# A hybrid convolution and attention encoder layer on one core: loads in halves, a first third of one projection inside attention, a split last block, two softmax blocks on ScalarE

## The chip, the cores and the metric

The kernel runs on one core of one Trainium2 chip. The metric is the device time of one execution in microseconds (us), compared as the median of several runs. The engines are named as in the profile: PE is TensorE's matmul, PEld its weight load, DVE is VectorE, ACT is ScalarE, POOL is GpSimd, SP issues the DMAs. L162 means line 162 of the kernel before.

## The reference, cut to what matters

The layer takes 528 prompt rows (16 learned meta rows and 512 frames) and 32 sample rows, so 560 rows of 1024 features, all in float32.

```python
x = x + 0.5 * ((silu(h @ w_gate) * (h @ w_up)) @ w_down)      # h = rms_norm(x), D_FF = 2816
z = rms_norm(x) @ w_in_all        # conv B | C | v | q latent | kv latent | rotary key | 2 gates
conv_branch = (B * dwconv3_causal(C * v)) @ w_conv_out
s = q @ k.T * 96 ** -0.5          # 16 heads, masked by chunks of 64
p = softmax(s)
mla_branch = (p @ v) @ w_mla_out
x = x + (sigmoid(g_conv) * conv_branch + sigmoid(g_mla) * mla_branch) @ w_out_all
x = x + 0.5 * ((silu(h @ w_gate2) * (h @ w_up2)) @ w_down2)
```

The outputs are the two row groups after the second feed-forward step and the new convolution and key caches.

## The kernel before, in words

Activations lie with features on the 128 partitions and rows along the free axis; 1024 features are KD = 8 tiles. Every float32 operand of a product is split into a rounded high part (a cast on ACT, L116) and the rest (a subtraction on DVE or POOL, L117 and L73), and `mm3` (L161 to L165) makes three matmuls of each product: high by high, low by high, high by low. The weights come in column blocks of 128, 512 KB each, by `load` (L119): one DMA on SP's queue, the cast, the subtraction.

There are five stages in the program.

1. **The start** (L613 to L656) loads the rows with SP, transposes them on PE, scales them with ACT and DVE into `xh` and `xl`, and loads the first block of the gate and up weights in two halves with `load_early` (L144). SP's queue holds the DMAs in the order in which they stand there: gains, first 128 prompt rows, meta rows, sample rows, second 128 prompt rows, then the halves of the weights, then the other prompt rows. The transposes of the first 304 columns need the first two prompt tiles and the sample and meta rows.
2. **Feed-forward step 1**, `ffn` (L235).
3. **The mix stage**: 16 heads of attention (loop at L1160), and in between, as filler, the units of `stream` (L929): the conv and gate columns of `w_in_all` and the product with `w_conv_out`. `fill(us)` (L962) draws units from it. The gates and the conv branch go to DRAM (`gt_dram`, `cb_dram`). Per head, `score` makes the logits in PSUM, `soft` (L1093) takes the maximum on DVE and the exponential on ACT, L1189 to L1191 divide the four blocks `pv(t)` of 528, 400, 272 and 144 columns by their sums on DVE, L1226 and L1231 transpose the weights, L1242 and L1243 multiply them by the values into `ov`, and L1246 and L1247 add the two halves into `at`. `sample_values` (L1102) does the same for the sample rows of a pair of heads. The attention result of the last pair of heads goes straight into `vh` and `vl` (L1253), the others by DRAM (L1216 to L1219).
4. **The late stage** (L1297 to L1330): eight blocks `m` of the product with `w_mla_out` (PSUM tile `late`), each multiplied by a sigmoid of its gate and added to the gated conv branch, then the eight blocks of `w_out_all`. The first of these matmuls stand behind all 16 heads.
5. **Feed-forward step 2**, the same `ffn`. At its end `down` (L443) makes eight blocks `m` of the product with `w_down`; `close` (L472) adds block `m` to `y`, `done` (L1364) then calls `emit(m - 1)` (L1348), which transposes a finished block back on PE, copies it on ACT and DVE and stores it. Block 7 is emitted after its own `close`.

The program text does not fix each engine's order. The build's scheduler decides it from the text's order, the dependencies and its own costs of instructions; `add_manual_dep` with NOSYNC forbids it to put one instruction ahead of another. Each engine's queue is then fixed and runs in order. PSUM tags in the mix stage are `t`, `f`, `acc` (two banks each) and `s` (one tile of two banks).

## Time and profile before

| | |
|---|---|
| median of 3 runs | 1419.42 us (1417.48 to 1420.46) |
| profiled execution, its own time | 1418.22 us |
| its span in the trace | 1416.40 us |
| PE / PEld busy | 1381.2 us (98%) / 1352.1 us (95%) |
| DVE / ACT / POOL busy | 1012.8 / 648.8 / 441.4 us |
| chain that ended last | PE 85%, DVE 6%, DMA 4%, ACT 2% |
| DMA | 141.62 MB, mean 100 GB/s |

The span is what the trace covers from the first to the last instruction or transfer; the execution's own time has 1.8 us around it. A busy matmul is modelled with its pipeline's drain, so the distance between the starts of neighbouring matmuls tells their cost, not their durations.

### The profile page before, as it was taken

How to read it: one execution, taken by the hardware profiler on the slowest of the kernel's cores; microseconds unless marked ns; L12 is line 12 of the kernel's file. 1: busy time of each engine (PE TensorE's matmuls, PEld its weight loads, DVE VectorE, ACT ScalarE, POOL GpSimd, SP SyncE). 2: the span in 40 equal slices, each digit the busy share in tenths (PEclk: the TensorE clock that was granted, in tenths of full speed). 3: DMA queues.
4: the chain of work that ended last, by engine and by line, in shares of the span. 5: the costliest groups of instructions: out<-in, count | busy, mean ns of one | idle time of the engine just before them, and what ended most of it. 6: DMA issues, size and time to landing. Idle time of an engine off the chain costs nothing.

```text
span 1416.4 us, 26510 instructions
## 1 busy us (share of the span) xinstructions
PE 1381.2 (98%) x10615; PEld 1352.1 (95%) x10615; DVE 1012.8 (72%) x1740; ACT 648.8 (46%) x1202; POOL 441.4 (31%) x647
## 2 busy tenths in 40 slices
PE   7999999999999999999999999999999999999998
PEld 6999999999999999999999999899999999999998
DVE  5887878787576666856965877545877787878754
ACT  6644343435324355564554556543545253434341
POOL 1011111112396864654533434032811111111110
PEclk9999999999999999999999999999999999999999
DMA  6342323233243222222432244355533332423213
GB/s 174 90 119 66 115 75 105 85 95 90 89 125 95 85 80 78 72 61 65 124 96 81 77 138 134 110 184 155 143 90 107 88 113 67 119 69 112 85 46 97
DMA packets 215633, 141.62 MB, mean 100 GB/s; under 512 B 6415, under 2 KB 202914, under 8 KB 215510
## 3 DMA queue, kind: packets, MB, share of 16 engines
q1 hardware_dynamic: 215510, 139.93, 33.5%
q8 instruction: 83, 1.36, 0.4%
q14 instruction: 40, 0.33, 0.1%
HBM read 124.15 MB, written 15.76 MB: 99 GB/s over the span
## 4 chain that ended last, share of the span: by engine, by line
PE 85%; DVE 6%; DMA 4%; ACT 2%; issue 2%; POOL 1%; SPq 0%; DVEq 0%; POOLq 0%; ACTq 0%
PE acc L162 8%; PE acc L164 8%; PE b L162 8%; PE acc L163 8%; PE b L163 8%; PE b L164 8%; PE f L162 6%; PE f L163 6%; PE f L164 6%; PE late L162 2%; PE late L164 2%; PE late L163 2%; DMA wr<-in_ffn_w_down_dram 2%; PE t L1242 1%; PE t L1226 1%
## 5 line engine op out<-in xcount | busy, mean ns | idle before, releaser
L116 ACT CAST wh<-wr 128x1024 fp32r<-128x1024 f32 (+2 forms) x166 | 167.8, 1018 | 271.0 <-PE acc L163 127.9
L73 POOL TENSOR_TENSOR al<-tu,ah 128x187 fp32r<-128x187 f32 (+3 forms) x108 | 95.6, 913 | 572.2 <-issue 342.5
L162 PE MATMUL f<-xh,wh 128*128 128x272 f32 (+1 forms) x816 | 239.6, 294 | 3.4 <-DVE ext L891 1.4
L164 PE MATMUL f<-xh,wl 128*128 128x272 f32 (+1 forms) x816 | 238.0, 292 | 0.0
L163 PE MATMUL f<-xl,wh 128*128 128x272 f32 (+1 forms) x816 | 237.9, 292 | 0.1
L162 PE MATMUL acc<-ah,wh 128*128 128x280 f32 (+1 forms) x704 | 203.2, 291 | 1.7 <-ACT wh L116 1.3
L163 PE MATMUL acc<-al,wh 128*128 128x280 f32 (+1 forms) x704 | 203.9, 291 | 0.0
L164 PE MATMUL acc<-ah,wl 128*128 128x280 f32 (+1 forms) x704 | 202.7, 290 | 0.0
L73 POOL TENSOR_TENSOR wl<-wr,wh 128x256 fp32r<-128x256 f32 x196 | 152.5, 808 | 141.4 <-ACT wh L116 113.1
L117 DVE TENSOR_TENSOR wl<-wr,wh 128x1024 fp32r<-128x1024 f32 (+2 forms) x116 | 138.0, 1199 | 42.7 <-ACT wh L116 34.6
L162 PEld LDWEIGHTS f<-xh,wh 128*128 128x128 f32 x816 | 153.9, 189 | 4.7 <-ACT wh L116 1.6
L163 PEld LDWEIGHTS f<-xl,wh 128*128 128x128 f32 x816 | 154.1, 189 | 1.0 <-DVE xl L117 0.3
L164 PEld LDWEIGHTS f<-xh,wl 128*128 128x128 f32 x816 | 154.0, 189 | 0.6
L163 PE MATMUL b<-xsl,yh 128*128 128x272 f32 (+1 forms) x468 | 135.7, 290 | 0.0
L162 PE MATMUL b<-xsh,yh 128*128 128x272 f32 (+1 forms) x468 | 135.7, 290 | 0.0
L164 PE MATMUL b<-xsh,yl 128*128 128x272 f32 (+1 forms) x468 | 135.1, 289 | 0.0
L162 PEld LDWEIGHTS acc<-ah,wh 128*128 128x128 f32 x704 | 131.9, 188 | 2.7 <-ACT wh L116 1.7
L163 PEld LDWEIGHTS acc<-al,wh 128*128 128x128 f32 x704 | 132.5, 188 | 0.0
L164 PEld LDWEIGHTS acc<-ah,wl 128*128 128x128 f32 x704 | 132.0, 188 | 0.2 <-DVE wl L117 0.2
L117 DVE TENSOR_TENSOR yl<-ws,yh 128x1024 fp32r<-128x1024 f32 x78 | 100.6, 1289 | 8.3 <-ACT yh L116 8.0
L474 DVE SCALAR_TENSOR_TENSOR tu<-acc,R 128x560 f32<-128x560 f32 (+1 forms) x80 | 58.2, 729 | 46.4 <-PE acc L164 46.0
L162 PE MATMUL b<-xh,wh 128*128 128x272 f32 (+1 forms) x312 | 90.5, 290 | 0.0
(359 smaller groups left out, 3811.4 us busy)
## 6 DMA issues: line engine op xcount, KB each, us to landing
wr<-in_w_in_all_dram SPq DMA_DIRECT2D x43, 512.0 KB, 4.0
wr<-in_ffn_w_down_dram SPq DMA_DIRECT2D x32, 512.0 KB, 3.6
wr<-in_ffn_w_gate_dram SPq DMA_DIRECT2D x24, 512.0 KB, 4.4
wr<-in_ffn_w_up_dram SPq DMA_DIRECT2D x23, 512.0 KB, 4.6
wq<-in_ffn_w_up_dram SPq DMA_DIRECT2D x20, 512.0 KB, 5.6
wq<-in_ffn_w_gate_dram SPq DMA_DIRECT2D x19, 512.0 KB, 3.9
wr<-in_ffn_w_down_dram SPq DMA_DIRECT2D x16, 384.0 KB, 3.4
gt_dram<-b SPq DMA_DIRECT2D x16, 272.0 KB, 2.0
```

The costliest lines, as they stand in the source:

```text
L73: last = op(out[:, lo:hi], a[:, lo:hi], b[:, lo:hi])
L116: a = S.copy(hi, src)
L117: return a, (E or V).tensor_sub(lo, src, f(hi))
L162: first = PE.matmul(out, a[0], b[0], start=start, stop=False, skip_group_check=onto)
L163: PE.matmul(out, a[0], b[1], start=False, stop=False, skip_group_check=onto)
L164: PE.matmul(out, a[1], b[0], start=False, stop=stop, skip_group_check=onto)
L474: V.scalar_tensor_tensor(t, ps[:, :, :n], 0.5, Rv, op0=ALU.mult, op1=ALU.mult)
L1226: PE.transpose(ps[:, (t - j) * P : (t - j + 1) * P], pw[:, a : a + P], ident)
L1242: PE.matmul(ov[:, 512 - NT[j] :], vj, x, start=j == 0 and x is pTh[j], stop=j == NQ - 1 and x is pTl[j])
```

## The change

There are four edits. **The rows come in halves of 512 features**: `load_early` issues the sample, meta and first two prompt tiles' first halves ahead of the first halves of the weights, and their second halves ahead of the second halves of the weights. **A first third of the product with `w_mla_out` moves into the mix stage**: for the blocks m = 0, 1, 2 `first_outs` multiplies the seven finished tiles k of `vh`, `vl` into the mix stage's own PSUM banks `s`, `acc` and `f`, behind the filler; `last_outs` adds the eighth k once the last pair of heads is done, with a weight tile `w_last` of its own, and multiplies by the gates. Their six gates and conv tiles are loaded, and their sigmoids taken, before the last head's weights are transposed, and never ahead of the last exponential. The last pair's `sample_values` moves from behind that head's values to ahead of its transposes. **The last block of the last product is split** into 416 and 128 columns; the first part is closed and emitted while the second runs. **Two of the four softmax blocks** (528 and 400 columns) are divided on ACT.

```diff
+    def load_early(ws, rows):
...
         for k0, k1, E in ((0, KD // 2, V), (KD // 2, KD, GP)):
+            rows(k0 * P, k1 * P)
             for w, (raw, hi, lo) in zip(ws, tiles):
...
+                if last and finale and m == KD - 1:
+                    done(m)
+                    for q, (c0, c1) in enumerate(((0, N2 - P), (N2 - P, N2))):
+                        out = ps[:, q, : c1 - c0]
+                        for j in range(nf):
+                            ah, al = a[pairs[j // 2]]
+                            mm3(
...
+                        t = rows()[:, c0:c1]
+                        yc = y[:, m, lo + c0 : lo + c1]
+                        V.scalar_tensor_tensor(
+                            t, out, 0.5, R[:, lo + c0 : lo + c1], op0=ALU.mult, op1=ALU.mult
+                        )
+                        V.tensor_add(yc, yc, t)
+                        finale(m, q)
+                    return
...
-            dma(xp[:, 0], i["x_prompt"][0, :P])
-            dma(xm[:META], i["meta_tokens"])
-            dma(xm[META:MS], i["x_sample"][0])
-            dma(xp[:, 1], i["x_prompt"][0, P : 2 * P])
-            w0 = load_early([wg[:, :P], wu[:, :P]])
+            def first_rows(c0, c1):
+                dma(xm[META:MS, c0:c1], i["x_sample"][0, :, c0:c1])
+                dma(xm[:META, c0:c1], i["meta_tokens"][:, c0:c1])
+                for t in range(2):
+                    dma(xp[:, t, c0:c1], i["x_prompt"][0, t * P : (t + 1) * P, c0:c1])
+
+            w0 = load_early([wg[:, :P], wu[:, :P]], first_rows)
...
+        def first_outs():
+
+            for m in range(AHEAD):
+                w = load([w_mla(m)[: (KD - 1) * P]], E=GP)
...
+                for k in range(KD - 1):
+                    for q in range(2):
+                        x = slice(q * NL, (q + 1) * NL)
+                        x = mm3(ps[q], at_k(w, k), at_k((vh, vl), k, x), k == 0, False)
+                        if k == 0 and m:
+                            behind(x, turned[NQ if m > 1 else 0])
+                        yield 0.345
+
+        def last_outs():
+            for m, ps in sorted(enumerate(outs), key=lambda x: x[0] < 2):
+                for q in range(2):
+                    x = slice(q * NL, (q + 1) * NL)
+                    mm3(ps[q], at_k(w_last, 0, slice(m * P, (m + 1) * P)), at_k((vh, vl), KD - 1, x), False, True)
+                    V.tensor_mul(gates[m][:, x], ps[q], gates[m][:, x])
+                V.tensor_add(gates[m], gates[m], convs[m])
...
+        AHEAD = 3
...
             for t in range(NQ - 1, -1, -1):
-                V.tensor_scalar_mul(pv(t), pv(t), inv[:, t : t + 1])
-            soft(nm, sm, 4, pss[rows, :KP], pS[rows], rows)
+                if t >= NQ - 2:
+                    S.activation(pv(t), pv(t), AF.Identity, scale=inv[:, t : t + 1])
+                else:
+                    V.tensor_scalar_mul(pv(t), pv(t), inv[:, t : t + 1])
+            last = soft(nm, sm, 4, pss[rows, :KP], pS[rows], rows)
...
+            if h == HEADS - 1:
+                sample_values(VV, at, pS)
...
-        fill(1e9)
+        for _ in chain(filler, first_outs()):
+            pass
+
+        for m in range(AHEAD):
+            sc = back.tile([P, L], F32, tag=f"raw{m}", name="sc")
+            dma(sc, gt_dram[m])
+            behind(S.activation(sc, sc, AF.Sigmoid), last)
+            dma(convs[m], cb_dram[m])
+            GP.tensor_mul(convs[m], convs[m], sc)
+            dma(gates[m], gt_dram[KD + m])
+            behind(S.activation(gates[m], gates[m], AF.Sigmoid), last)
+        last_outs()
...
-        for m in range(KD):
+        for m in range(AHEAD):
+            split(mh[:, m], ml[:, m], gates[m])
+        for m in range(AHEAD, KD):
...
+        def finale(m, q):
+            emit(m, *((0, 3), (3, 4))[q])
```

In the rows that follow the changed program's lines are its own: its L167 to L169 are `mm3`, L119 the cast of a split, L86 a DMA.

PE's queue at the end of the mix stage of the program before, from the last filler matmul on (`pw` are the last head's softmax weights, `pTh` and `pTl` their transposes, `VV` the values, `pM` and `VM` the meta keys' part):

```order
L164 MATMUL f<-xh,wl 128x272
L1226 MATMUL t<-ident,pw 128x128 x10
L1231 MATMUL t<-ident,pw 32x128 x4
L1242 MATMUL t<-pTh,VV 128x512
L1242 MATMUL t<-pTl,VV 128x512
L1242 MATMUL t<-pTh,VV 128x384
L1242 MATMUL t<-pTl,VV 128x384
L1242 MATMUL t<-pTh,VV 128x256
L1242 MATMUL t<-pTl,VV 128x256
L1242 MATMUL t<-pTh,VV 128x128
L1242 MATMUL t<-pTl,VV 128x128
L1243 MATMUL t<-pM,VM 64x512
```

The same queue in the changed program, from the last transposes of `pw`, a few rows of it:

```order
L1302 MATMUL t<-ident,pw 128x128
L167 MATMUL acc<-vh,wh 128x272
L168 MATMUL acc<-vl,wh 128x272
L169 MATMUL acc<-vh,wl 128x272
L1308 MATMUL t<-ident,pw 32x128 x4
L167 MATMUL f<-vh,wh 128x272
L168 MATMUL f<-vl,wh 128x272
```

The four groups of `pw` transposes, the meta columns' transposes, the `pTh` matmuls and the `pM` matmul stood back to back and now have 17 + 2, 14, 23, 3, 19 and 17 matmuls of `first_outs` (42 for each m) between them; the nine `VV,sTh` matmuls of `sample_values`, which stood behind them, stand ahead. Behind `pM` six are left, then one transpose, and then this:

```order
L1346 MATMUL t<-ident,ncv 32x128
L167 MATMUL f<-vh,wmh 128x272 x2
L167 MATMUL s<-vh,wmh 128x272
L167 MATMUL acc<-vh,wmh 128x272 x2
L168 MATMUL f<-vl,wmh 128x272
L169 MATMUL f<-vh,wml 128x272
```

These are `last_outs`: five matmuls that need only the high part of the last tile of attention results, then those that need its low part.

ACT's queue at the last head, in the program before and then in the changed one, from the exponential of the widest block (`pS` are the sample rows' weights, `sc` and `mixed` the gates, `b` a unit of the filler leaving its PSUM bank):

```order
L1098 ACTIVATE pw,sm<-s,nm 128x528
L924 COPY b_11187<-f 128x272
L1246 COPY at<-t 64x512
L1098 ACTIVATE pS,sm<-t,nm 32x288
L116 CAST wh<-wr 128x1024
```

```order
L1158 ACTIVATE pw,sm<-s,nm 128x528
L953 COPY b_11149<-f 128x272
L1253 ACTIVATE pw<-pw,inv 128x528
L1253 ACTIVATE pw<-pw,inv 128x400
L1323 COPY at<-t 64x512
L1158 ACTIVATE pS,sm<-t,nm 32x288
L1338 ACT_TABLE_LOAD
L1338 ACTIVATE sc<-sc 128x544
L1342 ACTIVATE mixed<-mixed 128x544
```

The two divisions stand behind the exponential in all 16 heads. The table load and six sigmoids, of which the last two rows are the first pair, stood in the late stage; now a cast, a copy out of `f` and the casts `sTh` for `sample_values` queue behind them.

SP's queue at the start, before and changed:

```order
L85 DMA craw<-in_ffn_norm_dram 8x128
L85 DMA xp<-in_x_prompt_dram 128x1024
L85 DMA xm<-in_meta_tokens_dram 16x1024
L85 DMA xm<-in_x_sample_dram 32x1024
L85 DMA xp<-in_x_prompt_dram 128x1024
L85 DMA wr<-in_ffn_w_gate_dram 128x4x128
L85 DMA wr<-in_ffn_w_up_dram 128x4x128
```

```order
L86 DMA craw<-in_ffn_norm_dram 8x128
L86 DMA xm<-in_x_sample_dram 32x512
L86 DMA xm<-in_meta_tokens_dram 16x512
L86 DMA xp<-in_x_prompt_dram 128x512 x2
L86 DMA wr<-in_ffn_w_gate_dram 128x4x128
L86 DMA wr<-in_ffn_w_up_dram 128x4x128
```

Ahead of the first weights there are still five DMAs, with half the bytes of the rows; the other four row DMAs stand behind these two, ahead of the weights' second halves.

## Rows read from the trace of the kernel before

**Rows 1.** Busy time by stage, the whole span (columns stand in the second line).
```profile
core 0: us, PE busy (x) PEld busy (x) DVE busy (x) ACT busy (x) POOL busy (x), PEclk, DMA share, GB/s
0.00:20.00 20.00, 12.99 (x60) 10.19 (x61) 6.13 (x14) 9.71 (x20) 3.70 (x12) 1.00 0.76 224
20.00:481.00 461.00, 455.85 (x3491) 450.79 (x3490) 351.62 (x542) 202.21 (x315) 127.86 (x189) 1.00 0.33 96
481.00:915.35 434.35, 427.90 (x3276) 412.66 (x3276) 300.52 (x709) 230.42 (x565) 206.78 (x324) 1.00 0.31 92
915.35:931.50 16.15, 11.08 (x61) 9.27 (x60) 6.17 (x13) 7.32 (x15) 0.00 (x0) 0.79 0.29 85
931.50:1405.13 473.63, 467.31 (x3691) 463.67 (x3689) 345.25 (x457) 197.35 (x286) 103.06 (x123) 1.00 0.37 107
1405.13:1416.40 11.27, 6.07 (x49) 5.53 (x46) 3.10 (x7) 1.76 (x3) 0.00 (x0) 0.98 0.25 74
```

**Rows 2.** Busy time of one stretch at the stage's border, columns as in rows 1.
```profile
925.00:931.00 6.00, 5.65 (x28) 5.23 (x27) 1.40 (x5) 2.19 (x3) 0.00 (x0) 0.50 0.23 62
```

**Rows 3.** Timeline of the program's end: start, duration, engine and instruction, idle before it.
```profile
1409.50 0.29 PE L163 MATMUL acc<-al,wh 128*128 128x272 f32 x1
1409.62 0.29 PE L164 MATMUL acc<-ah,wl 128*128 128x272 f32 x1
...
1413.12 0.39 SPq L85 DMA_DIRECT2D out_dram<-ot  x1
```

**Rows 4.** Timeline of the end of the mix stage, columns as in rows 3.
```profile
922.43 0.45 PE L1243 MATMUL t<-pM,VM 96*64 96x512 f32 x1 [0.81 <-ACT pM L1236]
...
922.91 0.58 ACT L1246 COPY at<-t 64x512 f32<-64x512 f32 x1 [0.54 <-PE t L1243]
...
923.52 0.69 DVE L1247 TENSOR_TENSOR at<-t,at 64x512 f32<-64x512 f32 x1 [1.76 <-ACT at L1246]
...
926.97 0.65 ACT L116 CAST vh<-at 128x544 fp32r<-128x544 f32 x1 [0.88 <-DVE at L1129]
...
927.65 0.73 DVE L117 TENSOR_TENSOR vl<-at,vh 128x544 fp32r<-128x544 f32 x1 [0.40 <-ACT vh L116]
```

**Rows 5.** Timeline of ACT in feed-forward step 1, a table load.
```profile
35.04 1.28 ACT L291 ACT_TABLE_LOAD   x1
```

**Rows 6.** Groups of instructions by line and form: busy us, mean ns, idle before.
```profile
L1191 DVE TENSOR_SCALAR pw<-pw,inv 128x528 f32<-128x528 f32 x16 | 9.1, 568 | 0.3
L1191 DVE TENSOR_SCALAR pw<-pw,inv 128x400 f32<-128x400 f32 x16 | 8.9, 554 | 0.0
...
L897 ACT ACTIVATE cv<-ext,cT 128x546 f32<-128x546 f32 x8 | 6.0, 748 | 4.8 <-DVE ext L893 4.8
L116 ACT CAST wh<-wr 128x1024 fp32r<-128x1024 f32 x43 | 45.1, 1048 | 31.3 <-PE f L163 20.1 <-PE f L164 5.6 <-issue 5.5
```

**Rows 7.** Timeline of the start, PE and ACT.
```profile
6.37 0.31 PE L633 MATMUL px<-ident,xm 48*128 48x48 f32 x1 [3.88 <-DMA xm<-in_x_sample_dram]
...
9.36 0.92 ACT L639 ACTIVATE xh<-px,cT 128x304 fp32r<-128x304 f32 x2 [5.30 <-PE px L636]
...
10.84 0.60 PE L162 MATMUL acc<-xh,wh 128*128 128x280 f32 x1 [0.88 <-ACT wh L116]
...
14.46 0.43 PE L164 MATMUL acc<-xh,wl 128*128 128x280 f32 x1
```

**Rows 8.** Timeline of the start, SP's queue, and a DMA group of the first 30 us.
```profile
3.01 0.43 SPq L85 DMA_DIRECT2D wr<-in_ffn_w_gate_dram  x1
...
wr<-in_ffn_w_gate_dram SPq DMA_DIRECT2D x2, 256.0 KB, 6.7
```

**Rows 9.** Timeline of the last head's value matmuls, PE.
```profile
921.28 0.22 PE L1242 MATMUL t<-pTh,VV 128*128 128x128 f32 x1
921.34 0.27 PE L1242 MATMUL t<-pTl,VV 128*128 128x128 f32 x1
```

**Rows 10.** One stretch inside attention, columns as in rows 1.
```profile
645.00:650.00 5.00, 3.86 (x32) 3.64 (x30) 4.79 (x13) 0.64 (x2) 2.82 (x5) 1.00 0.55 152
```

More of the change, by code (lines that the diff above doesn't have):

```diff
@@ L2 @@
 from functools import partial
+from itertools import chain
 import numpy as np
@@ L233, in summed, with ffn @@
         return gates, (xsh, xsl), [partial(combine, k) for k in range(KH)]
-    def ffn(pool, acc, one, wg, wu, wd, lo, y, R, w0, sums, before, done):
+    def ffn(pool, acc, one, wg, wu, wd, lo, y, R, w0, sums, before, done, finale=None):
         n = (T - lo) // 2
@@ L956, in stream, with behind @@
                 w = nxt
+        def first_outs():
+            for m in range(AHEAD):
+                w = load([w_mla(m)[: (KD - 1) * P]], E=GP)
+                if m == 0:
+                    t = psum.tile([P, 2, 512], F32, tag="s", name="s", bufs=1)
+                    ps = [t[:, q, :NL] for q in range(2)]
+                else:
+                    ps = [bank("acc" if m == 1 else "f")[:, :NL] for q in range(2)]
+                outs.append(ps)
+                for k in range(KD - 1):
[12 more added lines that the diff above has]
+                V.tensor_add(gates[m], gates[m], convs[m])
+        def behind(x, y):
+            tc.add_manual_dep(x.ins, y.ins.name, NOSYNC, reason="later")
+        AHEAD = 3
+        outs = []
         done_units = []
@@ L1214, in encoder_step @@
                 raws = [back.tile([P, L], F32, tag=f"raw{j}", name="raw") for j in range(3)]
+                mixed = [back.tile([P, L], F32, tag=f"mixed{j}", name="mixed") for j in range(2 * AHEAD)]
+                gates, convs = mixed[:AHEAD], mixed[AHEAD:]
+                w_last = load(
+                    [i["w_mla_out"][0, (KD - 1) * P :, : AHEAD * P]],
+                    [
+                        back.tile([P, AHEAD * P], d, tag=t, name=t)
+                        for d, t in ((F32, "raw0"), (F32R, "wmh"), (F32R, "wml"))
+                    ],
+                )
                 for k in range(KD - 1):
@@ L1230, in encoder_step @@
             for t in range(NQ):
[L1231 removed]
+                turned[NQ] = PE.transpose(
                     ps[:32, t * P : (t + 1) * P], pw[:, PO[t] : PO[t] + 32], ident
@@ L1369, in encoder_step @@
             pool, acc, one, i["ffn2_w_gate"][0], i["ffn2_w_up"][0], i["ffn2_w_down"][0],
-            META, y, R3, None, sums, before, done,
+            META, y, R3, None, sums, before, done, finale,
         )
```

53 lines of the change are left out of this document (33 added, 20 removed).

## The prediction

> **What bounds the kernel now.** I read the busy time by stage first, then the timeline where a stage loses time, then the groups of instructions. PE bounds the kernel: it is busy for 98% of the span, and the table by stage shows where the rest lies [rows 1]. Of 1416.4 us, PE is idle for 7.0 us in the first 20, 5.2 in the 461 us after that (the end of the start and feed-forward step 1), 6.4 in attention, 5.1 in the 16 us at the border to the late stage, 6.3 in the late stage and feed-forward step 2, and 5.2 after the last matmuls begin to run out. So a change that leaves the matmuls as they are can win little, and only at these places. The border stands out: 16.15 us hold 5.07 us of idle PE, and the granted clock has a mean of 0.79 there. DVE and ACT are idle for a third and more of every stage, so their work is cheap wherever it isn't the last thing that PE waits for.
>
> The sum below is made against the profiled execution, 1418.2 us by its own time; the median of the runs stands 1.2 us above it. About 0.2%, 2.8 us, is what a measurement of this kernel can tell from no change.
>
> **The border, the largest term.** Before, the last head's transposes, its value matmuls and the sample rows' part stand back to back on PE's queue, each waiting for a cast on ACT and a subtraction on DVE, and no other work is between. That costs twice. PE is idle for 16.15 - 11.08 = 5.07 us [rows 1]. And after this thin stretch the granted clock is 0.50, the lower of its two levels (1.2 GHz), for the six us from 925 to 931, in which PE is busy for 5.65 us [rows 2]; at the upper level the same matmuls would need half, so 2.8 us more are lost. Together 7.9 us. The change moves no matmul out of the program: it puts the 126 of `first_outs`, about 16 us of PE work at 0.125 us each (36 matmuls of 272 columns take the 4.49 us from 1405.13 to 1409.62 [rows 1, 3]), from behind this chain into its gaps. Between two neighbours of the chain 17 to 23 of them now stand at most places, 2 us and more, against gaps of 1 to 2 us.
>
> What stays open is the end of the chain, for the eighth tile of every product needs the last head. From the start of the `pM` matmul at 922.43 it takes ACT's copy and DVE's addition until 924.21, which is 1.78 us, then the cast into `vh` (0.65) and the subtraction into `vl` (0.73) [rows 4]: the high part is there after some 2.45 us, the low part after 3.2. To cover it PE has `pM` itself, six matmuls and one small transpose, about 1.1 us. So PE waits 1.35 us for the high part; the five matmuls that need only that take 0.6 us, and it waits another 0.15 for the low part. Of the 7.9 us 1.5 are lost again, and the gain is **6.4 us**. The small items (`w_last` is one DMA, one cast and one subtraction of 384 columns; the loads of six gates and conv tiles come earlier on SP's queue, three of them behind loads that they don't depend on) lie beside filler, with DMA at a share of 0.31 in that stage [rows 1], and I cost them at nothing. If that cover failed they would show as one wait of a sigmoid for its load.
>
> ACT could spoil this term. It takes the table load and six sigmoids in front of the casts for the sample rows and of a copy that frees a bank of `f`. The load is 1.28 us [rows 5]; a sigmoid of 544 columns isn't in these rows, so I take the 0.65 us of a cast of that size [rows 4]: 1.28 + 6 x 0.65 = 5.2 us, and with the weight cast behind them (1.05 [rows 6]) 6.2 us. PE has 38 + 3 + 4 + 25 + 1 matmuls from the sample scores to that point, some 8.5 us, so it should just be covered. Bounds for the border: 7.9 us if everything hides, 6.4 - 5.2 = 1.2 us if PE stands for all of it. I keep 6.4, near the upper end, because the cover is longer than the work.
>
> **The start.** The first matmul on a weight starts at 10.84, behind the cast of the weight, and ACT got the first transposed rows only at 9.36, while PE's first row transpose waited until 6.37 for the sample rows [rows 7]. The weight's first half is issued at 3.01 and takes 6.7 us to land [rows 8], because 1216 KB of rows are ahead of it. The change leaves 608 KB ahead. At the 224 GB/s of the first 20 us [rows 1] the other 608 KB are 2.8 us. The second halves are still behind all the same bytes and land as before, but they are needed some 5 us after the first, for PE runs its first matmuls slowly (0.43 us long at 14.46, against 0.29 at the end [rows 3, 7]). Bounds: nothing, if the second halves end the wait, and 2.8 us. I take **2.2 us**, near the upper end, since both things that PE waits for are late for the same reason. Prompt tiles 3 and 4 are issued later, and PE's first use of them is twice as far away.
>
> **The end.** The last block now costs more matmul time: 18 of 416 columns at 0.125 x 416 / 272 = 0.191 us are 3.4 us, and 18 of 128 columns cost between 0.06 us each, the distance of two such matmuls [rows 9], and the 0.125 us of the 272-column ones [rows 3], so 1.1 to 2.25 us; I take 1.4, near the row that has the same size. Block 6 is emitted ahead of the last 18 instead of behind them, five transposes, some 0.5 us. That is 5.3 us against 4.5, 0.8 us lost. Behind the last matmul, three operations of 512 to 544 columns shrink to 128; at 0.73 us for 544 columns on DVE [rows 4] each loses about 0.4 us, 1.2 us of the 3.5 from 1409.62 to the last DMA's issue at 1413.12 [rows 3]. The last transfer carries 64 KB instead of 256; 192 KB at 224 GB/s are 0.8 us. Net **1.2 us**, with bounds of 0.2 and 1.7.
>
> One rule of the Trainium skill speaks against this term. By "TensorE: Matmul & The Clock Gate", section "LDWEIGHTS (loading the stationary operand)", loading 128 columns takes P / 1.2 ns, 107 ns; as an estimate from that page the 18 narrow matmuls would need 1.9 us, and the term would be 0.7 us. The row of this size shows 0.06 us, but with the same weights loaded twice, so it does not settle it.
>
> **Two divisions on ACT.** DVE gets rid of 16 x (0.57 + 0.55) = 18 us of its 300 in attention [rows 1, 6]. ACT has no such row; its nearest one, 546 columns with a scale from SBUF, takes 0.75 us [rows 6], so 16 x (0.75 + 0.6) = 22 us come to its 230 of 434. The chain of a head gets no longer: two blocks on each engine side by side, 1.3 us, where DVE took four. Where PE is idle inside attention, DVE is what is full: from 645 to 650 PE loses 1.14 us while DVE is busy for 4.79 and ACT for 0.64 [rows 10]. Of the 6.4 us of the stage I take **1.0 us**, with bounds of 3 and, without a mishap, 0.
>
> **Sum.** 6.4 + 2.2 + 1.2 + 1.0 = 10.8 us, so 1418.2 - 10.8 = 1407.4; I say **1407.5 us**.
>
> **The rivals.**
> - *The second halves of the weights end the wait at the start*, and the 2.2 us are gone: 1409.6. For it: the same bytes are ahead of them. Against it: they have 5 us. Chance 0.14.
> - *The clock falls again*, or ACT's sigmoids hold PE up at the border. The wait of 1.5 us follows a stretch that is now full of matmuls, where before it followed eight thin us; if the clock went to its lower level all the same, the 2.8 us come back: 1410.2. A late ACT costs about the same. Chance 0.18.
> - *ACT becomes the wait of every head*: slower. ACT works in order, and the two divisions can stand behind a weight cast of 1.05 us [rows 6] while DVE has already done its two. PE then waits for the transposes' input. From 0.6 us a head (9.8 us over 16) it eats all the rest; at 1.05 us a head, with the attention term gone, it gives 1407.4 + 1.0 + 16.8 = 1425.2. For it: ACT needs more time for the same columns (0.75 against 0.57 us), and the casts sit on its queue. Against it: ACT is busy for 53% of the stage, DVE for 69%, and filler stands in front of the transposes. Chance 0.06. The Trainium skill ("ScalarE: Activation LUTs", section "Rules for kernel authors") says to put multiplications on VectorE, not ScalarE; by that rule alone this rival would be the forecast.
> - *The program does less than it says* (the scheduler puts the moved matmuls where they cover nothing). The order of the built program shows them in the gaps, so no chance of its own.
>
> **How the numbers follow.** The forecast has 0.62, the rivals 0.14, 0.18 and 0.06. The upper end of the range takes in the first two rivals together, 1407.4 + 2.2 + 2.8 = 1412.4, and a little of the end's bound: 1413. The lower end takes the best bounds, 7.9 + 2.8 + 1.7 + 3 = 15.4 us, less probable all at once: 1403. Faster by over 0.2% means below 1415.4: all but the slower rival and a part of worse mixtures, 0.92; within 0.2% 0.03; slower 0.05.
>
> **What would show it.** In the changed profile: the granted clock stays at 1.00 from the last head into the late stage; PE's only wait above 1 us there is for the cast into `vh`, 1 to 1.5 us; the first `acc` matmul starts between 8 and 9; the last block begins 5 to 6 us before the last matmul ends and the last store is issued some 2.3 us behind it; PE's idle time in attention is 5 to 6 us. It is wrong if the clock falls at the border, if PE waits there for `sTh` or a bank of `f`, or if waits of transposes for ACT's `pw` come back in many heads.

## The result, and the profile after

The changed kernel takes 1412.39 us (median of 6 runs, 1410.72 to 1414.43) against 1419.94 us: a ratio of 0.9950, with a 95% interval from 0.9939 to 0.9961. It is faster by 7.5 us, where 10.8 were forecast; when it was measured again beside the kernel before (below), by 5.8. The profiled execution is the slowest of the six, 1414.43 us with a span of 1412.60, so the two traces differ by only 3.8 us; a second profile of the same kernel (below) has a span of 1409.9, and the difference between the two teaches as much as either.

Busy time by stage of the changed kernel, columns as in rows 1; the border's stretch is 894.00 to 941.80 here, because 16 us of matmuls have moved into it:

```profile
0.00:20.00 20.00, 15.36 (x64) 13.06 (x65) 7.01 (x16) 10.27 (x21) 3.71 (x12) 1.00 0.74 223
20.00:481.00 461.00, 455.92 (x3487) 450.43 (x3486) 349.97 (x540) 201.28 (x313) 129.27 (x188) 1.00 0.33 96
481.00:894.00 413.00, 406.71 (x3106) 392.25 (x3104) 279.27 (x658) 237.20 (x572) 205.93 (x321) 1.00 0.32 97
894.00:941.80 47.80, 45.61 (x355) 44.02 (x354) 18.15 (x38) 24.76 (x52) 15.57 (x25) 1.00 0.34 104
941.80:1401.40 459.60, 452.05 (x3569) 448.33 (x3567) 340.22 (x453) 190.74 (x277) 97.60 (x114) 1.00 0.35 103
1401.40:1412.60 11.20, 7.17 (x49) 6.37 (x46) 3.21 (x9) 1.92 (x4) 0.00 (x0) 0.98 0.26 75
```

**The border** does what was forecast: the granted clock is 1.00 where it was 0.79 [rows 1] and 0.50 [rows 2], and the last head's transposes have no wait left. Two waits remain, on the timeline of PE, with the DVE and ACT rows that end them (start, duration, engine and instruction, idle before it):

```profile
936.55 0.27 PE L1346 MATMUL t<-ident,ncv 128*32 128x128 f32 x1
938.03 0.52 PE L167 MATMUL f<-vh,wmh 128*128 128x272 f32 x2 [1.21 <-ACT vh L119]
...
940.02 0.29 PE L169 MATMUL acc<-vh,wml 128*128 128x272 f32 x1
941.29 0.39 PE L167 MATMUL s<-vh,wmh 128*128 128x272 f32 x1 [0.98 <-DVE mixed L1010]
```
```profile
937.34 0.64 ACT L119 CAST vh<-at 128x544 fp32r<-128x544 f32 x1 [0.76 <-DVE at L1324]
```
```profile
940.81 0.43 DVE L1010 TENSOR_TENSOR mixed<-s,mixed 128x272 f32<-128x272 f32 x1
```

The first is the one that the forecast put at 1.35 us. The second was not in it: PE's matmul into the second half of tile `s` starts 0.05 us behind DVE's multiplication of the first half, which ends at 941.24.

**The start.** The first weight matmul starts at 7.48 instead of 10.84 [rows 7], 3.36 us earlier. But the matmuls of 280 columns then stand 0.23 us apart until 19.4, and 0.13 us only from there; before, the short distance began at 16.9. The granted clock is printed as 1.00 for these stretches, but the trace's record of it begins only at 16.6 us before and at 19.5 us here, so the views say nothing of it ahead of that; what state this is the warming matmuls show below. Of the 3.36 us only 0.91 are left where DVE first multiplies `b` by `kept` into `tu` in feed-forward step 1, at 62.91 against 63.82 before:

```profile
7.48 0.60 PE L167 MATMUL acc<-xh,wh 128*128 128x280 f32 x1 [0.47 <-ACT wh L119]
...
18.22 0.43 PE L167 MATMUL acc<-xh,wh 128*128 128x280 f32 x1
18.46 0.43 PE L168 MATMUL acc<-xl,wh 128*128 128x280 f32 x1
...
19.56 0.29 PE L169 MATMUL acc<-xh,wl 128*128 128x280 f32 x1
```
```profile
62.91 0.44 DVE L387 TENSOR_TENSOR tu<-b,kept 128x280 f32<-128x280 f32 x1
```

**The end.** PE and DVE in the split block, and the last store's issue:

```profile
1405.77 0.33 PE L167 MATMUL acc<-ah,wh 128*128 128x128 f32 x1 [0.19 <-DVE tu L517]
...
1407.49 0.28 PE L167 MATMUL acc<-ah,wh 128*128 128x128 f32 x1
1407.61 0.27 PE L168 MATMUL acc<-al,wh 128*128 128x128 f32 x1
1407.72 0.28 PE L169 MATMUL acc<-ah,wl 128*128 128x128 f32 x1
```
```profile
1408.60 0.29 DVE L517 SCALAR_TENSOR_TENSOR tu<-acc,R 128x128 f32<-128x128 f32 x1 [2.20 <-DMA out_dram<-ot]
```
```profile
1410.04 0.35 SPq L86 DMA_DIRECT2D out_dram<-ot  x1
```

The 18 narrow matmuls stand 0.11 us apart. DVE's last product starts 0.6 us behind the last matmul's end, at 1408.00, and the row names a store as what it waited for. From the start of block 6's last matmul to the end of the span it is 11.84 us, against 11.92 before: the split gained nothing. (The same split end takes 11.73 to 11.91 us in the other profiles.)

**Attention.** The waits of PE have moved together, and in this execution the clock fell behind them. Two rows of PE's timeline, then the stretch behind them in this profile and, below it, in the second profile of the same kernel (columns as in rows 1):

```profile
645.58 0.39 PE L167 MATMUL f<-xh,wh 128*128 128x274 f32 x1 [1.35 <-DVE b L938]
647.86 1.09 PE L1115 MATMUL acc<-ident,K 128*96 128x128 f32 x4 [0.88 <-DVE K L1066]
```
```profile
648.00:651.00 3.00, 3.00 (x15) 2.93 (x16) 2.51 (x5) 1.70 (x4) 0.60 (x1) 0.51 0.31 111
```
```profile
648.00:651.00 3.00, 3.00 (x26) 3.00 (x25) 2.65 (x6) 2.04 (x5) 0.00 (x0) 1.00 0.25 96
```

PE is as busy in both, with 15 instructions at 0.51 and 26 at 1.00.

### The profile page after: what moved, and what is told of

It is laid out like the page before. It is cut to its first block, busy times and chain, and to the rows that moved or that the text cites. A ratio compares the mean times of both kernels' runs of the same rounds, so it can differ in the third digit from the quotient of the medians.

```text
span 1412.6 us, 26502 instructions
## 1 busy us (share of the span) xinstructions
PE 1382.8 (98%) x10615; PEld 1354.5 (96%) x10615; DVE 997.8 (71%) x1711; ACT 666.2 (47%) x1236; POOL 452.1 (32%) x659
## 4 chain that ended last, share of the span: by engine, by line
PE 84%; DVE 6%; DMA 5%; ACT 3%; issue 2%; POOL 0%; SPq 0%; DVEq 0%; ACTq 0%
PE acc L167 9%; PE acc L169 9%; PE acc L168 9%; PE b L167 7%; PE b L168 7%; PE b L169 7%; PE f L167 7%; PE f L168 6%; PE f L169 6%; DMA wr<-in_ffn_w_down_dram 3%; PE late L167 2%; PE late L169 2%; PE late L168 2%; PE t L1319 1%; ACT wh L119 1%
## 5 line engine op out<-in xcount | busy, mean ns | idle before, releaser
L119 ACT CAST wh<-wr 128x1024 fp32r<-128x1024 f32 (+3 forms) x166 | 167.5, 1015 | 268.8 <-PE acc L168 128.8
L167 PE MATMUL f<-xh,wh 128*128 128x272 f32 (+1 forms) x816 | 240.4, 295 | 3.7 <-DVE ext L920 1.5
L169 PE MATMUL f<-xh,wl 128*128 128x272 f32 (+1 forms) x816 | 238.2, 292 | 0.0
L74 POOL TENSOR_TENSOR wl<-wr,wh 128x256 fp32r<-128x256 f32 (+1 forms) x208 | 161.7, 808 | 159.5 <-ACT wh L119 152.8
L167 PE MATMUL acc<-ah,wh 128*128 128x280 f32 (+2 forms) x704 | 203.6, 292 | 2.2 <-ACT wh L119 1.4
L168 PE MATMUL acc<-al,wh 128*128 128x280 f32 (+2 forms) x704 | 204.2, 291 | 0.0
L169 PE MATMUL acc<-ah,wl 128*128 128x280 f32 (+2 forms) x704 | 203.1, 291 | 0.1
L121 DVE TENSOR_TENSOR wl<-wr,wh 128x1024 fp32r<-128x1024 f32 (+2 forms) x113 | 134.2, 1197 | 40.3 <-ACT wh L119 33.0
L167 PEld LDWEIGHTS f<-xh,wh 128*128 128x128 f32 x816 | 154.1, 189 | 5.5 <-ACT wh L119 1.7
L169 PEld LDWEIGHTS f<-xh,wl 128*128 128x128 f32 x816 | 154.1, 189 | 0.6
L167 PE MATMUL b<-xsh,yh 128*128 128x272 f32 (+1 forms) x468 | 135.7, 290 | 0.0
L167 PEld LDWEIGHTS acc<-ah,wh 128*128 128x128 f32 x704 | 131.9, 188 | 3.8 <-ACT wh L119 2.4
L169 PE MATMUL b<-xsh,yl 128*128 128x272 f32 (+1 forms) x468 | 135.1, 289 | 0.0
L169 PEld LDWEIGHTS acc<-ah,wl 128*128 128x128 f32 x704 | 132.0, 188 | 0.4 <-DVE wl L121 0.3
L119 ACT CAST yh<-ws 128x1024 fp32r<-128x1024 f32 x78 | 81.5, 1045 | 19.5 <-PE b L168 15.1
L167 PE MATMUL b<-xh,wh 128*128 128x272 f32 (+1 forms) x312 | 90.5, 290 | 0.0
```

Source lines behind the costliest of these rows:

```text
L74: last = op(out[:, lo:hi], a[:, lo:hi], b[:, lo:hi])
L119: a = S.copy(hi, src)
L121: return a, (E or V).tensor_sub(lo, src, f(hi))
L167: first = PE.matmul(out, a[0], b[0], start=start, stop=False, skip_group_check=onto)
L168: PE.matmul(out, a[0], b[1], start=False, stop=False, skip_group_check=onto)
L169: PE.matmul(out, a[1], b[0], start=False, stop=stop, skip_group_check=onto)
```

## The experiments

Two distances on PE's timeline put the edits side by side. One is the **start**: when DVE first multiplies `b` by `kept` into `tu`, the last row of the start above. The other is the **mix stage**: from the end of PE's wait for `ext` at its beginning (484.55 before, 484.71 after) to the end of its wait for `y` in feed-forward step 2 (1026.34 and 1021.32). In the kernel before, and with the border undone, three matmuls of that step stand ahead of the wait for `y`; in all the others they stand behind it, and the wait is longer. So for equal work 0.4 us have to be taken off those two figures. The wait for `y`, before and then changed:

```profile
1026.34 0.36 PE L162 MATMUL acc<-xh,wh 128*128 128x272 f32 x1 [0.53 <-DVE y L1327]
```
```profile
1021.32 0.36 PE L167 MATMUL acc<-xh,wh 128*128 128x272 f32 x1 [0.91 <-DVE y L1420]
```

The last column says where in attention the granted clock fell to some 0.5.

| kernel | median, us | ratio to before (95%) | start | mix stage | clock fell at |
|---|---|---|---|---|---|
| before (by call) | 1418.26 to 1419.94 | | 63.82 | 541.79 | not |
| changed | 1412.39 | 0.9950 (0.9939 to 0.9961) | 62.91 | 536.61 | 648 |
| changed, again | 1412.74 | 0.9958 (0.9947 to 0.9970) | 62.06 | 535.15 | not |
| rows whole | 1415.05 | 0.9969 (0.9956 to 0.9981) | 63.86 | 536.61 | 693 |
| division on DVE | 1412.60 | 0.9956 (0.9943 to 0.9968) | 62.09 | 537.34 | not |
| division on ACT in the last head only | 1414.32 | 0.9966 (0.9954 to 0.9978) | 62.90 | 537.54 | not |
| border undone | 1414.93 | 0.9971 (0.9960 to 0.9983) | 63.46 | 539.34 | 648 |
| last block whole | 1413.11 | 0.9962 (0.9949 to 0.9974) | 62.98 | 536.58 | 648 |
| warming matmuls | 1410.17 | 0.9949 (0.9937 to 0.9961) | 62.33 | 535.11 | not |
| own tiles at the end | 1413.16 | 0.9965 (0.9953 to 0.9976) | 63.08 | 536.22 | 693 |
| both halves first | 1411.74 | 0.9951 (0.9939 to 0.9963) | 62.76 | 535.85 | 648 |
| the last three together | 1412.11 | 0.9947 (0.9931 to 0.9964) | 61.34 | 536.99 | 648 |
| the same, ACT in the last head only | 1414.55 | 0.9963 (0.9950 to 0.9976) | 61.99 | 538.97 | not in attention, at 940 |

With intervals of 0.1 to 0.2% to either side, the medians settle only steps of some 2 us; smaller ones are read from the traces, which show one execution each; the two of the changed kernel differ by 0.85 us at the start and by 1.46 in the mix stage.

**Rows whole.** `first_rows` is gone, and the rows are loaded as before.

```diff
-            w0 = load_early([wg[:, :P], wu[:, :P]], first_rows)
+            dma(xp[:, 0], i["x_prompt"][0, :P])
...
+            w0 = load_early([wg[:, :P], wu[:, :P]], lambda c0, c1: None)
```

> The changed kernel with the first edit undone: the first rows are loaded whole again, ahead of the weights; all else as changed. The forecast's theory (the start gains 2.2 us): the time goes up by 2.2 us to some 1414.6. The rival from the changed profile (the first weight matmul is 3.4 us earlier, but the matmuls keep their double pitch until 19.4 us instead of 16.7, so nearly all is given back): up by 0 to 0.9 us, 1412.4 to 1413.3; in its profile the first weight matmul at about 10.8 and the short pitch from about 16.7.

The first weight matmul is at 11.17, the short distance begins at 17.1, and the start is at 63.86, as before. In the kernels with halved rows and no warming it is at 62.06 to 63.46, and their short distance begins anywhere from 16.6 to 19.6. (The 63.46, with the border undone, has a fall of the clock in it: from 27 to 30 us the granted clock reads 0.50.) So at this point the halves keep 0.4 to 1.8 us of the 3.4 that the first matmul gains. By the end of step 1 the traces show nothing of it: the wait for `ext` ends at 484.40 in this run and at 484.55 in the kernel before, and at 483.28 to 485.40, with a middle value of 484.36, in the nine profiles with halved rows and no warming. On the way, at 345 us, PE waits 0.17 to 1.11 us in six of these nine for a weight whose cast starts 5.6 to 6.6 us after its issue; with whole rows it starts after 4.5 and 5.5 us and PE does not wait. Whether the halved rows have to do with that is not shown. By the medians the halves are worth 2.3 to 2.7 us, by the ratios 1.6 to 2.7, with an error of more than 1 us. So the traces are with the theory of the late clock, the medians alone would leave the forecast standing, and what this edit is worth stays open.

**Division on DVE.**

```diff
-                if t >= NQ - 2:
-                    S.activation(pv(t), pv(t), AF.Identity, scale=inv[:, t : t + 1])
-                else:
-                    V.tensor_scalar_mul(pv(t), pv(t), inv[:, t : t + 1])
+                V.tensor_scalar_mul(pv(t), pv(t), inv[:, t : t + 1])
```

> The changed kernel with all four softmax blocks divided on VectorE again. The forecast's theory (attention gains 1.0 us by the move): up by 1.0 us to 1413.4. The rival (PE is idle in attention for as long as before, 6.2 us in the waits of over 0.25 us in both, so the move is worth nothing): 1412.4, within 0.5 us. The slower rival (ScalarE holds heads up): below 1412.

The median is the same. The trace shows that this sameness is a sum: the clock doesn't fall in attention, and the wait for `vh` at the border is 1.77 us instead of 1.21, with another of 0.53 ahead of it. The mix stage is 0.73 us longer than in the changed kernel's first profile and 2.19 longer than in its second.

**The last block whole**, in two runs. The first of them left the call that emits block 7 where the program already had one.

```diff
-                if last and finale and m == KD - 1:
+                if False:
...
+        emit(KD - 1)
```

> The changed kernel with the last block of the last product whole again, closed and emitted as before. The forecast's theory (the split gains 1.2 us): up to 1413.6. The rival from the changed profile (the narrow matmuls stand 0.111 us apart, not 0.077, and two new waits of about 0.3 and 0.55 us stand in the split block, so the split gains next to nothing): 1412.4 to 1412.7.

It took 1414.44 us, 0.9972 (0.9961 to 0.9984), with block 7 transposed and stored twice; its time has a doubled end in it and says nothing of the split. The second run is without the last line.

> The changed kernel with the last block of the last product whole again, as before; the run e3_unsplit also emitted that block a second time, some 2 us of its own at the end, so its time doesn't count. The forecast's theory (the split gains 1.2 us): 1413.6. The rival (narrow matmuls 0.111 us apart and two new waits of 0.3 and 0.55 us eat it): 1412.4, within 0.5 us; from the last matmul of block 6 to the end of the span 11.8 to 11.9 us, as with the split (11.8).

From block 6's last matmul to the end it is 11.90 us, against 11.84 with the split. The rival is confirmed: the split is worth nothing here.

**Border undone.** `AHEAD` is 0, all eight blocks stand in the late stage, and `sample_values` behind the last head.

```diff
-        AHEAD = 3
+        AHEAD = 0
...
-        for _ in chain(filler, first_outs()):
-            pass
+        fill(1e9)
...
-        last_outs()
```

> The changed kernel without the move of the first third of the product with w_mla_out: all eight blocks in the late stage, the last sample_values behind the last head, as before. The forecast's theory (the border gains 6.4 us): up to 1418.8, with the granted clock at 0.50 for some six us behind the border and 5 us of idle PE there. By the two traces the border gains some 5.2 us (7.9 less waits of 1.21 and 0.98 us and small ones): 1417.6. If the border's gain came from elsewhere: below 1415.

Only some 2.5 us are lost, which is just inside what was expected if the border's gain came from elsewhere (below 1415). A part of it does. The border's clock falls again, but for a shorter stretch than before [rows 2], and its chain waits less, 1.97, 1.17 and 0.35 us instead of 5.07 in all [rows 1]:

```profile
924.00:927.00 3.00, 2.65 (x15) 2.37 (x14) 1.45 (x5) 1.65 (x3) 0.00 (x0) 0.58 0.01 1
927.00:930.00 3.00, 3.00 (x23) 3.00 (x22) 0.00 (x0) 0.54 (x1) 0.00 (x0) 0.85 0.55 167
```

With the two divisions on ACT, DVE is no longer late at the last head's transposes. So the edits overlap. By the mix stage the border alone (division on DVE) is worth 541.79 - 537.34 = 4.45 us, or 4.1 with the 0.4 named above taken off; the division alone (border undone) 2.45; and both together 5.18, or 4.8. The last two have a fall of the clock in attention in them.

**Warming matmuls.** Six matmuls on zeros while PE waits for its first data.

```diff
+            zero = pool.tile([P, 512], F32, tag="tg", name="zero", bufs=3)
+            V.memset(zero, 0.0)
...
+                    PE.matmul(pz, zero[:, :P].bitcast(F32R), zero.bitcast(F32R), start=True, stop=True)
```

> The changed kernel with six matmuls of 512 columns on a tile of zeros at the very start, ahead of every row transpose, while PE waits for the first DMAs; their result is never read. The theory of the late clock (the start's gain is lost because PE's matmuls keep the double pitch, 0.235 us for 280 columns, until it has worked for a while): the short pitch comes earlier, before 14 us rather than at 16 to 19, and the time falls by 2 to 4 us, to 1408.4 to 1410.4. The rival (the double pitch has another cause at the start, or ScalarE, busy without a pause from 8 to 15 us, is the limit there): 1412.4, within 0.7 us.

PE's timeline in this run:

```profile
1.46 2.93 PE L643 MATMUL pz<-zero 128*128 128x512 f32 x6 [1.46 <-DVE ss L656]
...
11.02 0.29 PE L167 MATMUL acc<-xh,wh 128*128 128x280 f32 x1
11.15 0.29 PE L168 MATMUL acc<-xl,wh 128*128 128x280 f32 x1
...
21.64 0.53 PE L167 MATMUL acc<-xh,wh 128*128 128x280 f32 x2 [2.18 <-ACT xh L674]
```

The short distance is there by 11.0, eight us sooner. So at the start the long distance does come from PE's work so far, and the forecast's row of 0.43 us at 14.46 [rows 7] was that state and no property of the matmul. Most of the gain ends at 21.64: ACT stands at a cast for a weight that is there at 20.16, with `xh` behind it, and PE waits 2.18 us. Behind this wait the long distance comes back, and here the granted clock is on record, at 0.50:

```profile
24.00:27.00 3.00, 3.00 (x12) 2.37 (x10) 2.04 (x10) 3.00 (x9) 0.00 (x0) 0.50 1.00 237
```
```profile
24.87 0.43 PE L168 MATMUL acc<-xl,wh 128*128 128x280 f32 x1
25.11 0.43 PE L169 MATMUL acc<-xh,wl 128*128 128x280 f32 x1
```

The rows are those of the start, 0.43 us long and 0.23 us apart, so the state at the start is the lower of the clock's two levels (1.2 GHz), and the record of the clock begins where PE leaves it. By the trace 0.6 us stay against the changed kernel's first profile (62.33 against 62.91), none against its second (62.06). The median says 1410.17, but its interval covers the changed kernel's.

**Own tiles at the end.**

```diff
+                        if q:
+                            ps = acc()
                         out = ps[:, q, : c1 - c0]
...
-                        t = rows()[:, c0:c1]
+                        t = pool.tile([P, P], F32, tag="last", name="tl") if q else rows()[:, c0:c1]
```

> The changed kernel, but the second part of the split last block gets a PSUM tile of its own and an SBUF tile of its own for its scaled sum. If the two waits in the split block come from sharing tiles (PE's first narrow matmul waits for VectorE's read of the other half of the same PSUM tile, VectorE's last product for the store of block 6 out of the buffer it takes): both go, and the end gets 0.8 us shorter: 11.0 us from the last matmul of block 6 to the end of the span against 11.8, 1411.6 us in all. If they have other causes: 11.8 and 1412.4.

The end is 11.57 us: 0.3 less, not 0.8. Both waits go, as the rows show, and a third comes:

```profile
1406.23 0.28 PE L169 MATMUL acc<-ah,wl 128*128 128x128 f32 x1
...
1406.54 0.29 DVE L519 SCALAR_TENSOR_TENSOR tl<-acc,R 128x128 f32<-128x128 f32 x1 [0.29 <-PE acc L169]
...
1408.41 0.27 ACT L1456 COPY ot<-b 128x128 f32<-128x128 f32 x1 [0.93 <-DMA out_dram<-ot]
```

The tiles `tu` and `ot` share two buffers. With `t` out of them, the last `ot` gets the buffer that block 6's store still reads. That settles the cause of the wait at 1408.60, and that it isn't cured by moving one user.

**Both halves first.**

```diff
                 for q in range(2):
                     x = slice(q * NL, (q + 1) * NL)
                     mm3(ps[q], at_k(w_last, 0, slice(m * P, (m + 1) * P)), at_k((vh, vl), KD - 1, x), False, True)
+                for q in range(2):
+                    x = slice(q * NL, (q + 1) * NL)
                     V.tensor_mul(gates[m][:, x], ps[q], gates[m][:, x])
```

> The changed kernel, but last_outs writes both halves of a block's product before VectorE multiplies either by its gate. If PE's wait of 0.98 us ahead of the last three matmuls of block 0 comes from the order of the text (the second half goes into the same PSUM tile that VectorE is still reading): the wait goes, the time falls by some 0.9 us to 1411.5, and the border keeps only the wait of 1.2 us for vh. If VectorE's product is late for another reason, a wait of about the same size shows elsewhere before the first late matmul and the time stays at 1412.4.

The wait of 0.98 us is gone, and ahead of the first `late` matmul 0.25 us come in its place; the mix stage is 0.76 us shorter than in the profile of the changed kernel, both with a fall of the clock at 648. So the order of the text made that wait:

```profile
939.15 0.29 PE L167 MATMUL s<-vh,wmh 128*128 128x272 f32 x1
...
940.45 0.39 PE L167 MATMUL late<-vh,wh 128*128 128x272 f32 x1 [0.25 <-DVE mixed L1012]
```

**The changed kernel again.**

> The changed kernel once more, as the measure for the other three on this chip and for what differs from execution to execution: 1412.4 us, within 1; in its profile the first weight matmul at 7.5, the start's double pitch ending anywhere from 16 to 19.5 us, and in attention either a stretch of some 3 us at the lower clock behind two waits close together (at about 648 or 693 us) or none.

The same program, the same waits in attention (1.34 and 0.87 us at 645 to 647, 0.79 and 1.13 at 689 to 691), and no fall of the clock. The mix stage is 535.15 us instead of 536.61, so the fall costs 1.46 us; by the other profiles whose mix stage has the same program (536.22 to 536.61 with a fall, 535.11 without) 1.1 to 1.5. Among the ten profiles of kernels that divide on ACT in all heads the clock fell in eight, at 648 or 693; among the four that don't, the kernel before with them, in none.

**Division on ACT in the last head only.**

```diff
-                if t >= NQ - 2:
+                if t >= NQ - 2 and h == HEADS - 1:
```

> The changed kernel, with the two wide softmax blocks divided on ScalarE in the last head only; in the other 15 heads VectorE divides all four, as before. If the move earns at the border alone (the last head's chain gets shorter), and in attention saves some 1.5 us of waits and gives 1.45 us back by a fall of the clock: the wait for vh stays 1.2 us, no fall of the clock in attention, waits there as before (1.09, 1.14, 1.29, 1.32 us), and the time is that of the changed kernel within 0.7 us. If the move earned 1.0 us in attention, as forecast: up by 1 us, 1413.4.

Neither of the two came: the wait for `vh` is 1.77 us, as with the division on DVE, and the mix stage is no shorter than there (537.54 and 537.34). The division on the last head alone gains nothing; in this build only three matmuls, not six, stand between `pM` and `last_outs`. What the other 15 heads do is shown by the stretches of attention, first in this kernel, then in the changed one's second profile:

```profile
590.00:640.00 50.00, 48.91 (x382) 47.01 (x381) 31.28 (x83) 27.59 (x69) 26.91 (x46) 1.00 0.27 76
640.00:715.00 75.00, 72.53 (x550) 70.04 (x549) 58.41 (x134) 35.96 (x85) 39.16 (x62) 1.00 0.33 96
715.00:890.00 175.00, 173.43 (x1332) 166.34 (x1331) 118.82 (x283) 93.51 (x240) 65.65 (x97) 1.00 0.38 117
```
```profile
590.00:640.00 50.00, 49.99 (x388) 48.01 (x387) 31.16 (x82) 31.25 (x76) 25.97 (x46) 1.00 0.27 77
640.00:715.00 75.00, 70.28 (x525) 66.86 (x523) 55.85 (x123) 37.11 (x88) 41.61 (x61) 1.00 0.32 90
715.00:890.00 175.00, 175.00 (x1355) 168.77 (x1354) 117.33 (x282) 103.84 (x258) 67.79 (x97) 1.00 0.38 119
```

The move clears PE's idle time from 590 to 640 (1.09 us to 0.01) and from 715 to 890 (1.57 to 0.00), and adds 2.25 us from 640 to 715. DVE is busy there for 58.41 and 55.85 of the 75 us, and around the waits (644 to 648) for 3.86 and 3.93 of four in both kernels; why PE waits longer for a DVE with less to do stays open. That is 0.4 us in all; the waits at the border (1.77, 1.10 and 0.53 us here, 1.21 and 0.98 there) make 1.2 more of the 2.39 between the two mix stages, and the rest isn't found in single waits.

**The edits together**, with the last `ot` in a tile of its own too, and the same with the division on ACT in the last head only.

```diff
-            ot = pool.tile([P, n, P], F32, tag="tu", name="ot", bufs=2)
+            ot = pool.tile([P, n, P], F32, tag="tu" if n > 1 else "lot", name="ot", bufs=2 if n > 1 else 1)
```

> The changed kernel with the warming matmuls, both halves of a block ahead of the multiplications in last_outs, and in the split last block a PSUM tile, a tile for the sum and a tile for the last store of its own. By the single traces: the start some 0.5 to 1 us shorter, the border 1.0, the end 0.6 to 0.9 (from the last matmul of block 6 to the end of the span 11.0 to 11.2 us against 11.8), so 1409.5 us, between 1409 and 1411. If the parts eat one another (the next wait is as long): 1411.5 or more.

> The last but one kernel's edits together with the division on ScalarE in the last head only. If the fall of the clock in attention comes in most executions, this is as fast as the kernel with all the edits or up to 0.7 us faster; if it comes in few, it is up to 1.5 us slower than that one.

Neither beats the changed kernel clearly: 1412.11 (1406.73 to 1415.71) and 1414.55 against 1412.74 beside them. For the first this is what was expected if the parts eat one another; the second misses its forecast, 2.4 us slower where at most 1.5 were expected. The end is 11.48 us in both, all three waits gone. But the warming brought something else in the first one's profile: PE ran at the upper level by 7.7, then waited 0.90 and 0.36 us for `xh` and `xl`, and the granted clock fell until 14.9, as the stretch shows:

```profile
9.00:12.00 3.00, 3.00 (x14) 2.64 (x13) 2.13 (x5) 2.94 (x8) 0.49 (x1) 0.50 1.10 352
```

The start was still the earliest of all (61.34), but at the wait for `ext` (483.67) no more than 0.7 us of that is left against the middle of the nine above. In the mix stage it has the fall at 648 and a wait of 0.78 us at 867 that no other profile has; why is open. The version for the last head only takes 2.4 us more by the median and 1.98 by the mix stage, but its profile also has a wait of 1.29 us for ACT at 851.85 that no other has. Its simpler pair took 1.6 more than the changed kernel beside it by the median and 2.4 by the mix stage. Each median is within its error; together they speak for keeping the division in all heads.

## Why the prediction was right, and where its terms were not

The direction came out as forecast, and so did the mechanism of the largest term. 1412.4 lies in the range of 1403 to 1413, but near its upper end, and there by some luck: that end was put so far up for two rivals that did not occur, and the 3.3 us that are missing of the 10.8 went elsewhere.

1. **The border: 6.4 forecast.** Right were the clock at 1.00, the cover of the chain, ACT's work and the loads that cost nothing (PE is busy for all of the 30 us from 905 to 935, the row below), and the price of the wait for `vh`, 1.21 against 1.35. The rival that the clock falls again at the border, or that the sigmoids hold PE up, did not occur; they took 0.64 to 0.66 us each, as taken. Three things failed. The step "it waits another 0.15 for the low part" took the rest of `last_outs` to flow; it misses the wait of 0.98 us that the order of the text puts between a multiplication and the other half of its tile. And the 5.07 us of idle time were taken as this edit's alone, though the division on ACT shortens the same chain. And the wait for `y` at the beginning of feed-forward step 2 grew from 0.53 to 0.91, for the three matmuls of that step no longer stand ahead of it; the forecast looked no further than the border. Alone the border earns 4.1 us: with the division on DVE its waits are 1.77, 1.08 and 0.53, and 7.9 - 3.4 - 0.4 = 4.1.

```profile
905.00:935.00 30.00, 30.00 (x239) 29.20 (x238) 8.54 (x19) 16.18 (x31) 9.90 (x17) 1.00 0.35 105
```

2. **Two divisions on ACT: 1.0 forecast.** Beside the border they earn 2.2 us where the clock stays and 0.7 where it falls, so by the traces the size holds (the medians show no difference), but for another reason: more than half of it comes at the border. "Where PE is idle inside attention, DVE is what is full" was a good guide in two of the three stretches, 2.65 us; from 640 to 715 DVE was full too, but relieving it did not help, and the waits there are longer and closer together. That these would bring the clock down for 1.46 us was in no rival. ACT's rows are as taken, 0.74 us for 528 columns and 0.62 for 400, so the slower rival (ACT late in every head) never came near:

```profile
L1253 ACT ACTIVATE pw<-pw,inv 128x528 f32<-128x528 f32 x16 | 11.8, 737 | 1.3 <-DVE inv L1250 1.2
...
L1253 ACT ACTIVATE pw<-pw,inv 128x400 f32<-128x400 f32 x16 | 9.9, 616 | 0.0
```

   So the rule of "ScalarE: Activation LUTs", section "Rules for kernel authors", in the Trainium skill, which would have kept this multiplication on VectorE, did not decide here: the wide blocks take 0.17 and 0.06 us longer on ACT [rows 6], and it is the engine with time to spare.
3. **The start: 2.2 forecast, 0.4 to 1.8 in the traces at 62 us, nothing at the end of step 1.** The bytes gave more than thought, 3.36 us at the first matmul, and the second halves of the weights never held PE up in the changed kernel, so that rival is out. The step that failed is "they are needed some 5 us after the first, for PE runs its first matmuls slowly": it used the slow matmuls as a cover and did not ask whether they would stay slow for longer when they begin sooner. They did, from 7.5 to 19.4 where it had been from 10.8 to 16.9.
4. **The end: 1.2 forecast, 0.08 measured**, less than its lower bound of 0.2. The tail behind the last matmul shrank as said, though it has a wait of 0.6 us for a shared buffer in it: the last store is issued 2.32 us behind it, against 3.50 [rows 3]. But from block 6's last matmul to the last one it is 6.93 us instead of 5.09, so 1.84 were lost and not 0.8. PE waited some 0.35 us for the other half of the tile (1405.30 to 1405.77, where neighbours stand 0.11 apart), and the narrow matmuls were put at 1.4 us and took 2.0, at 0.11 us each. The row of 0.06 us [rows 9] is the first step behind wider matmuls; the next one is 0.11 there too. That the pair has the same weights, as the prediction says, is not the reason: of three neighbours in the split block the first two have the same `wh` and stand 0.11 apart like the others, and matmuls of 128 columns whose weights have only 64 columns stand 0.06 apart, the same weights or not (the last two rows):

```profile
933.21 0.22 PE L1319 MATMUL t<-pTh,VV 128*128 128x128 f32 x1
933.27 0.28 PE L1319 MATMUL t<-pTl,VV 128*128 128x128 f32 x1
933.38 0.34 PE L168 MATMUL f<-vl,wh 128*128 128x272 f32 x1
```
```profile
917.10 0.22 PE L168 MATMUL t<-VV,sTh 128*64 128x128 f32 x1
917.15 0.22 PE L169 MATMUL t<-VV,sTl 128*64 128x128 f32 x1
```

   The rule of "TensorE: Matmul & The Clock Gate", section "LDWEIGHTS (loading the stationary operand)", in the Trainium skill, 107 ns to load 128 columns, agrees with the 111 ns of this trace; it was the better guide.

With the sizes of the traces the sum is 0 to 1.8 for the start, 4.8 to 6.3 for the mix stage (with and without a fall of the clock) and 0.1 for the end, so 4.9 to 8.2 us; the 7.5 and the 5.8 measured both lie in it. The two profiled executions differ by less because the steps with no edit in them, feed-forward steps 1 and 2, took some 1 us longer each in the changed kernel's profile. They vary by that much between profiles. From the start's row to the wait for `ext` it takes 420.5 and 420.7 us in the two profiles with whole rows and 421.1 to 422.3 in all twelve with halved ones; whether that is the start's gain given back or the chance of late weights stays open.

## What to carry to other kernels

Where PE is busy for 98%, an edit is worth what its stage's waits are worth, and two edits that shorten the same chain share one gain: cost them together. A matmul into one half of a PSUM tile can wait for the reader of the other half, and a new user of a rotating buffer for a store; look for such neighbours in the text before a small tail is split. Count a wait's effect on PE's clock with the wait, and ask of a start that is moved ahead at which level of the clock PE will run it.

## What the runs showed of the hardware

- At the start PE's matmuls of 280 columns stand 0.23 us apart instead of 0.13. It is the distance at the lower level of the clock: in a stretch at 24 to 27 us of the run with warming, where the granted clock is recorded as 0.50, they stand 0.23 us apart too. The trace's record of the clock begins where the short distance does (16.6 us before, 19.5 in the changed kernel), and a view of an earlier stretch prints 1.00. With the first weight matmul between 7.4 and 7.8, the short distance came anywhere from 16.6 to 19.6 us in profiles of kernels with the same start. With six matmuls on zeros ahead it was there by 11.0 in one execution; in two others PE waited some 0.36 us for `xl` behind the first weight matmul, and the granted clock read 0.50 until 14.9 and 11.9.
- Behind two waits of 1.35 and 0.88 us that end 2.3 us apart the granted clock was 0.51 for some 3 us in one execution, and stayed at 1.00 in another of the same program. A fall cost 1.1 to 1.5 us.
- 128-column matmuls with weights of 128 columns stand 0.11 us apart in a series, neighbours with the same weights too; only the first step behind wider matmuls is 0.06 us [rows 9]. With weights of 64 columns they stand 0.06 us apart.
